# Moving three steps of an attention trunk by one slot: the value product, the sums of squares, the last heads

## The chip, the cores and the metric

The kernel runs on one core of one Trainium2 chip. Its engines are TensorE (PE: matmuls, transposes by matmul), ScalarE (ACT), VectorE (DVE), GpSimd (POOL) and SyncE (SP), which starts the transfers. Each engine works through its own queue in order. The metric is the time of one execution on the device in microseconds; lower is better.

## What is computed

Two pre-norm residual layers over 512 positions of width 2048, in float32. Layer 0 is an attention in which a small indexer scores all causal keys and each query attends to the best 128. Layer 1 is a block attention, which at this length comes to plain causal attention over 512 keys. Both have 16 query heads of width 128 that share 4 key and value heads, with a norm and a rotation of queries and keys, and a gate. Cut to what matters:

```python
def dsa_mixer(h, w_in, q_g, k_g, w_out):
    q, k, v, gate, qi, ki, wi = split_cols(h @ w_in, A_WIDTHS)
    q = rope(rms_norm(q.reshape(B, T, N_HEADS, HEAD_DIM), q_g), pos)
    k = rope(rms_norm(k.reshape(B, T, N_KV_HEADS, HEAD_DIM), k_g), pos)
    ...
    logits = jnp.einsum('bqgrd,bqkgd->bqgrk', qb, k_sel).astype(jnp.float32) * scale
    logits = jnp.where(valid[:, :, None, None, :], logits, NEG)
    p = jax.nn.softmax(logits, axis=-1).astype(v.dtype)
    o = jnp.einsum('bqgrk,bqkgd->bqgrd', p, v_sel)
    ...
    return (jax.nn.silu(gate) * o) @ w_out
```

## The kernel before

**The grid of slots.** All large matmuls are projections. Each makes a tile of 128 output columns (one head of `q`, `k`, `v` or the gate `g`, or 128 columns of an output projection `o0_n`, `o1_n`) for all 512 positions, and is cut into four quarters of four input tiles. A quarter is a unit: `products` (L184) issues 12 matmuls for it, since each float32 factor is split into a high and a low part and three products are kept (L193 high by high, L194 high by low, L195 low by high). The main loop goes over 484 units; the index of the unit is the slot. In slot i it splits the weights of unit i + 2 (`split`, L172: ACT casts the high part `whi`, DVE or GpSimd subtracts the low part `wlo`; three buffers each), starts loads, issues the 12 matmuls of unit i, perhaps starts the scores of a head (`maybe_attend`, L531), and then runs what was set for this slot with `later(k, f)`, that is k slots after the call.

**What sets the order.** On TensorE and SP the program's order stands as written. On ACT, DVE and GpSimd a scheduler orders the instructions after the opening part, so there a step can stand before or after its neighbours of other slots.

**Tiles and their steps.** When the four quarters of a tile are done, `done` sets its steps. A key tile (`k_tile`, L302) squares the result and cuts the squares into three bf16 parts (`Norm`, names `sq`, `b`), sums them over the head by 12 small matmuls (`sums`, name `cs`), makes the scale (`s3`, GpSimd's power), turns it into rows by four transposes (`bcast`, L224, name `b_k`), and multiplies the rotated keys by it (`s5`, DVE, name `t_k`), which then are cut into `kh` and `kl`. A query tile (L371) does the same without the row step: its scale `sc` goes into the softmax, so the scores need `q` alone, and the softmax needs `sc`. A value tile (L343) is scaled and then turned by four transposes (`s2`, L355, name `tv_v`). In each of the four groups of a layer a key tile, a value tile and four query tiles follow each other, with the gates between.

**One small bank.** `psm` (L123) gives the results of `sums`, `bcast` and the value tile's transposes a tile with the tag `sm`, which has one buffer.

**A head.** `attend` (L434) issues 12 score matmuls. Counted in slots from there: softmax at 1 (`soft`: on DVE the mask, `S<-s,mask`, on ACT the exponent), the division and a 32 by 32 turn on DVE at 2 (`u`), a transfer out at 3 and back at 4 (`leave`, `back`, names `d`, `pt`), the casts into `ph` (ACT) and `pl` (DVE) at 6, the value product `pv` (15 matmuls, L512, name `o`) at 8, the gate (`og`) at 9 and its low part at 10. `u` and `ph` share a tag with one buffer. The scores of a head start four slots or more after its query tile is done and 7 or 8 slots after those of the head before.

Of the kernel before, what the change touches and what calls it, by code (L numbers as in the profile page):

```python
# [37 lines left out]
HEADS = 16  # L38
# [55 lines left out]
def build(tc, a):  # L94
# [15 lines left out]
    def t512(tag, name, dt=F32, bufs=None, p=None, cols=T):  # L110
        return (p or kp).tile([P, cols], dt, tag=tag, name=name, **({"bufs": bufs} if bufs else {}))
# [4 lines left out]
    def small(tag, name, bufs=2):  # L116
        return kp.tile([P, NQ], F32, tag=tag, name=name, bufs=bufs)
# [13 lines left out]
    now = [0]  # L131
    SPLIT = 2

    def later(k, f, first=False):
        fs = hooks.setdefault(now[0] + k, [])
        fs.insert(0 if first else len(fs), f)
# [62 lines left out]
    def add(t, quarters=range(4)):  # L199
        units.extend((t, q) for q in quarters)  # L200
# [23 lines left out]
    def bcast(col, name):  # L224

        t = psm(name)
        for j in range(NQ):
            nc.tensor.transpose(t[:, j * P:(j + 1) * P], col[:, j:j + 1].to_broadcast([P, P]), ident)
        return t

    def cut_hi(hi, src):
        nc.scalar.copy(hi, src)

    def cut_lo(lo, src, hi):
        dve.tensor_tensor(lo, src, hi.bitcast(F32), op=OP.subtract)
# [28 lines left out]
    def rope(z, g, name):  # L264

        t1 = tmp(f"t1_{name}")
        t2 = tmp(f"t2_{name}")
        dve.scalar_tensor_tensor(t1, z, g, cos, op0=OP.mult, op1=OP.mult)
        for o, i in ((0, 64), (64, 0)):
            dve.scalar_tensor_tensor(t2[o:o + 64], z[i:i + 64], g[i:i + 64], sin[i:i + 64],  # L270
                                           op0=OP.mult, op1=OP.mult)
        dve.tensor_tensor(t1, t1, t2, op=OP.add)
        return t1
# [28 lines left out]
    def k_tile(Y, g):  # L302
        n = f"k{Y.L}_{g}"
        early = Y.L == 0 and g == 1
        v = SimpleNamespace()

        def s1():
            v.n = Norm(v.z, n)
            v.r = rope(v.z, Y.kg, n)

        def s2():
            v.n.middle()

        def s2b():
            v.s = v.n.sums()

        def s3():
            u = small("u", f"u_{n}")
            dve.scalar_tensor_tensor(u, v.s, 1.0 / P, Y.ce, op0=OP.mult, op1=OP.add)
            v.rk = small("rk", f"rk_{n}", 1)  # L320
            gps.tensor_tensor(v.rk, u, mhalf, op=OP.pow)

        def s4():
            v.b = bcast(v.rk, f"b_{n}")

        def s5():
            dve.tensor_tensor(v.r, v.r, v.b, op=OP.mult)
            p, th, tl = (bp, "bh15", "bl15") if early else (kp, "kh", "kl")
            kh = t512(th, f"kh_{n}", F32R, p=p)
            kl = t512(tl, f"kl_{n}", F32R, p=p)  # L330
            cut_hi(kh, v.r)
            Y.K[g] = (kh, kl)

        def s6():
            cut_lo(Y.K[g][1], v.r, Y.K[g][0])

        def done(z):
            v.z = z
            for k, f in ((1, s1), (2, s2), (3, s2b), (4, s3), (5, s4), (6, s5), (7, s6)):
                later(k, f)  # L340
        add(Tile(n, Y.w[16 + g], Y.X, done))

    def v_tile(Y, g):  # L343
# [27 lines left out]
    def q_tile(Y, h):  # L371
        n = f"q{Y.L}_{h}"
        early = Y.L == 0 and h < 8
        v = SimpleNamespace()

        def s1():
            v.n = Norm(v.z, n)
            v.r = rope(v.z, Y.qg, n)

        def s2b():  # L380
            v.s = v.n.sums()

        def s2():
            v.n.middle()
            p, th, tl = (bp, f"bh{9 - h % 4}", f"bl{9 - h % 4}") if early else (kp, "qh", "ql")
            qh = t512(th, f"qh_{n}", F32R, p=p)
            ql = t512(tl, f"ql_{n}", F32R, p=p)
            cut_hi(qh, v.r)
            cut_lo(ql, v.r, qh)
            Y.q[h] = (qh, ql)  # L390

        def s3():
            u = small("u", f"u_{n}")
            dve.tensor_tensor(u, v.s, Y.cq, op=OP.add)
            sc = small("sc", f"sc_{n}", 6)
            gps.tensor_tensor(sc, u, mhalf, op=OP.pow)
            Y.sc[h] = sc

        def done(z):
            v.z = z  # L400
            Y.qslot[h] = now[0]
            for k, f in ((1, s1), (2, s2), (3 + early, s2b), (4 + early, s3)):
                later(k, f)
        add(Tile(n, Y.w[h], Y.X, done))

    def g_tile(Y, h):
# [27 lines left out]
    def attend(Y, h):  # L434
# [53 lines left out]
        def cuts(hi, lo):  # L488
            if 0 in hi:
                v.ph = t512("ph", f"ph{n}", F32R, cols=1280)  # L490
                v.pl = t512("pl", f"pl{n}", F32R, cols=1280)
            for i in hi:
                o = slice(640 * i, 640 * i + 640)
                cut_hi(v.ph[:, o], v.t[:, o])
            for i in lo:
                o = slice(640 * i, 640 * i + 640)
                cut_lo(v.pl[:, o], v.t[:, o], v.ph[:, o])
# [27 lines left out]

        later(1, soft, True)
        for k, f in ((2, norm), (2, turn), (3, leave), (4, back),
                     (6, lambda: cuts((0, 1), (0, 1))), (8, pv), (9, gate), (10, rest)):
            later(k, f)

    def maybe_attend(Y):  # L531
        h = Y.head
        apart = 7 if h >= HEADS - 2 or (Y.L == 0 and h < 12) else 8
        if h < HEADS and Y.open and h in Y.qslot and now[0] >= Y.qslot[h] + 4 and now[0] >= Y.slot + apart:
            Y.head, Y.slot = h + 1, now[0]
            attend(Y, h)

# [281 lines left out]
    for i in range(len(units)):  # L819
        now[0] = i  # L820
        if i == OPENING:
            opening.close()
        dve.slot(i * SLOT)
        gps.slot(i * SLOT)
        if i in (2, 4):
            take_x(i // 2 + 1)
        split(i + SPLIT)
        if i == 0:
            take_x(1)
        if i in (0, 1):  # L830
            load(i + SPLIT, 1)
            load_x(i + 2)
        load(i + SPLIT)
        if i == 1:
            for n, t in (("cosi", cosi), ("sini", sini), ("cos", cos), ("sin", sin)):
                nc.sync.dma_start(t, a[n])
        products(i)
        maybe_attend(A if i < second else B)
        pending = hooks.get(i, [])
        while pending:  # L840
            pending.pop(0)()
        while fill and dve.until < (i + 1) * SLOT - SPARE:
            fill.pop(0)()
    for i in sorted(k for k in hooks if k >= len(units)):
        now[0] = i
        maybe_attend(B)
        for f in hooks[i]:
            f()
# [51 lines left out]
```

## Time and profile before

| | us |
|---|---|
| time, median of 3 runs | 1522.53 (1520.85 to 1524.11) |
| the profiled execution's own time | 1524.55 |
| its span, first to last instruction | 1522.8 |
| busy: TensorE, DVE, ACT, GpSimd | 1488.4, 916.5, 694.9, 145.5 |

The profile is of one execution. The busy times say which engine the span is made of. The table of waits says how long an engine sat idle and what ended that. The timeline has instructions in order of time: the start, how long it took, engine, line, operation, out<-in, and in square brackets the idle time before it and who ended it. A timeline row that ends in xN merges N instructions. Matmuls overlap, so the distance of two starts is what one costs, not its length. PEclk is the granted clock of TensorE, 1.00 for 2.4 GHz and 0.50 for 1.2 GHz. The lines L77 on DVE and GpSimd are a helper that issues all their operations: there the names tell them apart.

### The profile page before, as it was taken

To read this page: it belongs to the slowest core of one execution; us is meant where nothing else is said; L and a number is where in the kernel's file an instruction comes from. 1 tells how busy PE (TensorE), PEld (TensorE's weight loads), DVE (VectorE), ACT (ScalarE), POOL (GpSimd) and SP (SyncE) were. 2 spreads that over 40 slices of the span, in tenths; PEclk is the share of its full clock that TensorE was granted. 3 is DMA by queue.
4 is the path that set the end of the run, shared out by engine and by line. 5 is a ranking of instruction groups with operands and counts; after the bars stand their busy time and mean duration, and the time that the engine had idled before them with its cause. 6 is when DMAs were issued, how large, how long until landed. Compare 5 with 4: busy or idle time off the path is not lost.

```text
span 1522.8 us, 20238 instructions
## 1 busy us (share of the span) xinstructions
PE 1488.4 (98%) x7348; PEld 1243.2 (82%) x7348; DVE 916.5 (60%) x1848; ACT 694.9 (46%) x1332; POOL 145.5 (10%) x128
## 2 busy tenths in 40 slices
PE   9999999999998999999999999999999999999999
PEld 6998888878777788888888888888888888888887
DVE  5898966665666556653334565667666666643332
ACT  6874334544455435443333454455444545542221
POOL 0433540000000000001111000000000000000000
PEclk9999999999999999999999999999999999999999
DMA  7332224343344424354443244343425343354442
GB/s 244 106 97 84 85 96 139 118 142 115 108 135 128 128 70 135 115 180 145 146 145 132 84 135 136 114 121 104 153 84 152 104 132 104 122 156 166 145 145 90
DMA packets 72677, 191.79 MB, mean 126 GB/s; under 512 B 8192, under 2 KB 25344, under 8 KB 72576
## 3 DMA queue, kind: packets, MB, share of 16 engines
q1 hardware_dynamic: 72576, 190.50, 39.8%
q8 instruction: 57, 0.93, 0.3%
q14 instruction: 44, 0.36, 0.1%
HBM read 161.11 MB, written 29.36 MB: 125 GB/s over the span
## 4 chain that ended last, share of the span: by engine, by line
PE 64%; ACT 2%; DVE 1%; issue 1%; DVEq 0%; ACTq 0%
PE z_o L193 8%; PE z_o L195 8%; PE z_o L194 8%; PE z_g L193 5%; PE z_q L193 5%; PE z_q L194 5%; PE z_g L195 5%; PE z_g L194 5%; PE z_q L195 5%; PE o L512 3%; PE z_v L193 1%; PE z_k L193 1%; PE z_k L194 1%; PE z_k L195 1%; PE z_v L195 1%; PE z_v L194 1%
## 5 line engine op out<-in xcount | busy, mean ns | idle before, releaser
L193 PE MATMUL z_q<-xh,whi_q 128*128 128x512 f32 x512 | 203.8, 398 | 0.0
L193 PE MATMUL z_g<-xh,whi_g 128*128 128x512 f32 x512 | 202.7, 396 | 0.0
L195 PE MATMUL z_q<-xh,wlo_q 128*128 128x512 f32 x512 | 200.7, 392 | 0.0
L194 PE MATMUL z_q<-xl,whi_q 128*128 128x512 f32 x512 | 200.7, 392 | 0.0
L195 PE MATMUL z_g<-xh,wlo_g 128*128 128x512 f32 x512 | 199.8, 390 | 0.0
L194 PE MATMUL z_g<-xl,whi_g 128*128 128x512 f32 x512 | 199.3, 389 | 0.0
L193 PE MATMUL z_o<-bh,whi_o 128*128 128x512 f32 x512 | 199.3, 389 | 0.0
L195 PE MATMUL z_o<-bh,wlo_o 128*128 128x512 f32 x512 | 199.2, 389 | 0.0
L194 PE MATMUL z_o<-bl,whi_o 128*128 128x512 f32 x512 | 199.2, 389 | 0.0
L77 DVE TENSOR_TENSOR wlo_o<-raw_o,whi_o 128x512 fp32r<-128x512 f32 x128 | 88.8, 694 | 159.6 <-ACT whi_o L179 159.6
L179 ACT CAST whi_o<-raw_o 128x512 fp32r<-128x512 f32 x128 | 79.8, 624 | 225.6 <-PE z_o L194 215.9
L179 ACT CAST whi_g<-raw_g 128x512 fp32r<-128x512 f32 x128 | 79.4, 620 | 172.3 <-PE z_q L194 122.8
L179 ACT CAST whi_q<-raw_q 128x512 fp32r<-128x512 f32 x128 | 79.3, 620 | 159.1 <-PE z_q L194 74.2
L77 DVE TENSOR_TENSOR wlo_g<-raw_g,whi_g 128x512 fp32r<-128x512 f32 x112 | 76.7, 686 | 107.2 <-ACT whi_g L179 106.9
L77 DVE TENSOR_TENSOR wlo_q<-raw_q,whi_q 128x512 fp32r<-128x512 f32 x114 | 77.6, 684 | 63.9 <-ACT whi_q L179 58.7
L195 PEld LDWEIGHTS z_q<-xh,wlo_q 128*128 128x128 f32 x512 | 96.8, 189 | 20.9
L195 PEld LDWEIGHTS z_g<-xh,wlo_g 128*128 128x128 f32 x512 | 96.1, 188 | 20.9
L194 PEld LDWEIGHTS z_q<-xl,whi_q 128*128 128x128 f32 x512 | 97.1, 190 | 19.1
L193 PEld LDWEIGHTS z_q<-xh,whi_q 128*128 128x128 f32 x512 | 97.1, 190 | 19.0
L195 PEld LDWEIGHTS z_o<-bh,wlo_o 128*128 128x128 f32 x512 | 96.1, 188 | 20.1
L194 PEld LDWEIGHTS z_o<-bl,whi_o 128*128 128x128 f32 x512 | 96.1, 188 | 20.1
L193 PEld LDWEIGHTS z_o<-bh,whi_o 128*128 128x128 f32 x512 | 96.1, 188 | 19.6
(167 smaller groups left out, 2733.3 us busy)
## 6 DMA issues: line engine op xcount, KB each, us to landing
d<-u SPq DMA_DIRECT2D x32, 640.0 KB, 3.2
pt<-d SPq DMA_DIRECT2D x128, 160.0 KB, 4.0
raw_q<-w_a SPq DMA_DIRECT2D x32, 512.0 KB, 3.9
raw_g<-w_a SPq DMA_DIRECT2D x32, 512.0 KB, 3.9
raw_q<-w_b SPq DMA_DIRECT2D x32, 512.0 KB, 3.7
raw_g<-w_b SPq DMA_DIRECT2D x32, 512.0 KB, 3.6
raw_o<-w_ao SPq DMA_DIRECT2D x26, 512.0 KB, 3.6
raw_o<-w_bo SPq DMA_DIRECT2D x26, 512.0 KB, 3.6
```

What stands on the lines that cost most here:

```text
L77: return f(out, *args, **kw)
L179: nc.scalar.copy(hi, r)
L193: nc.tensor.matmul(o, lhsT=hi[:, k], rhs=xh, start=kt == 0, stop=False)
L194: nc.tensor.matmul(o, lhsT=hi[:, k], rhs=xl, start=False, stop=False)
L195: nc.tensor.matmul(o, lhsT=lo[:, k], rhs=xh, start=False, stop=kt == KT - 1)
L512: nc.tensor.matmul(o[:, q], lhsT=l[:, kt * P:kt * P + P], rhs=r[:, t], start=m == 0 and c == 0, stop=m == 4 and c == 2)
```

## The change

The steps of a key tile after the cutting of squares move one slot later (sums 4, scale 5, rows 6, product 7, low part 8); the sums and the scale of a query tile stand at 4 and 5, where the first eight query tiles of layer 0 stood already. Scores start five slots or more after their query tile instead of four. The value product stands nine slots after the scores instead of eight, gate and low part follow. The last three heads instead of the last two are seven slots apart.

```diff
         def done(z):
             v.z = z
-            for k, f in ((1, s1), (2, s2), (3, s2b), (4, s3), (5, s4), (6, s5), (7, s6)):
+            for k, f in ((1, s1), (2, s2), (4, s2b), (5, s3), (6, s4), (7, s5), (8, s6)):
                 later(k, f)
         add(Tile(n, Y.w[16 + g], Y.X, done))
...
             Y.qslot[h] = now[0]
-            for k, f in ((1, s1), (2, s2), (3 + early, s2b), (4 + early, s3)):
+            for k, f in ((1, s1), (2, s2), (4, s2b), (5, s3)):
                 later(k, f)
...
         for k, f in ((2, norm), (2, turn), (3, leave), (4, back),
-                     (6, lambda: cuts((0, 1), (0, 1))), (8, pv), (9, gate), (10, rest)):
+                     (6, lambda: cuts((0, 1), (0, 1))), (9, pv), (10, gate), (11, rest)):
             later(k, f)
...
-        apart = 7 if h >= HEADS - 2 or (Y.L == 0 and h < 12) else 8
-        if h < HEADS and Y.open and h in Y.qslot and now[0] >= Y.qslot[h] + 4 and now[0] >= Y.slot + apart:
+        apart = 7 if h >= HEADS - 3 or (Y.L == 0 and h < 12) else 8
+        if h < HEADS and Y.open and h in Y.qslot and now[0] >= Y.qslot[h] + 5 and now[0] >= Y.slot + apart:
```

On ACT, around the casts `ph` of head 5 in layer 0, whose value product stood after unit `k0_2_2` and now stands after `k0_2_3` (the two units before `v0_2_0`), there was this row:

```order
L415 ACTIVATE th_g0_7_3753<-gz_g0_7_3751 128x512
L179 CAST whi_k0_2_3_3755<-raw_k0_2_2_3566 128x512
L179 CAST whi_v0_2_0_3790<-raw_v0_2_0_3671 128x512
L179 CAST whi_v0_2_1_3838<-raw_v0_2_0_3671 128x512
L232 CAST ph0_5_3745<-pt0_5_3662 128x640 x2
L460 ACTIVATE S0_6_3806,sm0_6_3807<-S0_6_3806,nb0_6_3809,sc_q0_6_3387 128x512
```

and on the same engine and place there is now:

```order
L415 ACTIVATE th_g0_7_3753<-gz_g0_7_3751 128x512
L179 CAST whi_k0_2_3_3755<-raw_k0_2_2_3566 128x512
L179 CAST whi_v0_2_0_3790<-raw_v0_2_0_3666 128x512
L232 CAST ph0_5_3745<-pt0_5_3657 128x640 x2
L179 CAST whi_v0_2_1_3822<-raw_v0_2_0_3666 128x512
L179 CAST whi_v0_2_2_3868<-raw_v0_2_2_3714 128x512
```

`ph` moved ahead of one cast of weights, and the product that reads it moved back by one unit.

On TensorE, at the third key tile of layer 1, whose scale is turned into rows by `b_k1_2`, the matmuls stood in this order (`tv_v1_2`, the value tile's transposes, came after nine more matmuls of `z_q1_8`):

```order
L195 MATMUL z_q1_8_10283<-xh1_3_6695,wlo_q1_8_0_10213 128x512
L228 MATMUL b_k1_2_10301<-ident_80,rk_k1_2_10277 128x128 x4
L193 MATMUL z_q1_8_10283<-xh1_4_6775,whi_q1_8_1_10241 128x512
L194 MATMUL z_q1_8_10283<-xl1_4_6776,whi_q1_8_1_10241 128x512
L195 MATMUL z_q1_8_10283<-xh1_4_6775,wlo_q1_8_1_10242 128x512
```

and now, after the value product of head 7:

```order
L512 MATMUL o1_7_10300<-pl1_7_10223,vh_v1_1_9132 128x256
L512 MATMUL o1_7_10300<-pl1_7_10223,vh_v1_1_9132 128x128
L228 MATMUL b_k1_2_10316<-ident_80,rk_k1_2_10278 128x128 x4
L355 MATMUL tv_v1_2_10321<-ident_80,vt_v1_2_10280 128x128 x4
L193 MATMUL z_q1_8_10263<-xh1_8_7107,whi_q1_8_2_10259 128x512
```

The two sets of transposes, both into the tag `sm`, moved next to each other; so they stand at all eight key tiles.

On DVE, ahead of the product `t1_k0_2` of the third key tile of layer 0, which reads `b_k0_2`, there stood:

```order
L77 SCALAR_TENSOR_TENSOR u_k0_2_3983<-cs_k0_2_3946,ce0_1380 128x4
L77 TENSOR_TENSOR vt_v0_2_4024<-z_v0_2_3877,rstd0_1448 128x512
L77 TENSOR_TENSOR wlo_q0_8_2_3988<-raw_q0_8_2_3842,whi_q0_8_2_3987 128x512
L77 TENSOR_TENSOR wlo_q0_8_3_4027<-raw_q0_8_2_3842,whi_q0_8_3_4026 128x512
L77 TENSOR_TENSOR t1_k0_2_3899<-t1_k0_2_3899,b_k0_2_4019 128x512
L77 TENSOR_TENSOR pl0_6_3978<-pt0_6_3872,ph0_6_3977 128x640 x2
```

and now:

```order
L77 TENSOR_TENSOR wlo_q0_9_0_4066<-raw_q0_9_0_3908,whi_q0_9_0_4065 128x512
L77 ISA S0_7_4039,mx0_7_4041<-s0_0_7_4000,mask_93 128x512
L77 ISA mx0_7_4041 128x1
L77 ISA S0_7_4039,mx0_7_4041<-s1_0_7_4001,mask_93 128x384
L77 ISA mx0_7_4041 128x1
L77 SCALAR_TENSOR_TENSOR nb0_7_4042<-mx0_7_4041,sc_q0_7_3644 128x1
L77 ISA S0_7_4039,mx0_7_4041<-s1_0_7_4001,mask_93 128x128
L77 ISA mx0_7_4041 128x1
L77 SCALAR_TENSOR_TENSOR nb0_7_4042<-mx0_7_4041,sc_q0_7_3644 128x1
L77 ISA S0_7_4039,mx0_7_4041<-s2_0_7_4002,mask_93 128x256
L77 TENSOR_TENSOR t1_k0_2_3898<-t1_k0_2_3898,b_k0_2_4055 128x512
```

The masking of the scores of head 7 moved ahead of the key tile's product.

## Rows read from the trace of the kernel before

**Rows 1.** The page: busy time, share, instructions; the chain of waits by engine.

```profile
PE 1488.4 (98%) x7348; PEld 1243.2 (82%) x7348; DVE 916.5 (60%) x1848; ACT 694.9 (46%) x1332; POOL 145.5 (10%) x128
PE 64%; ACT 2%; DVE 1%; issue 1%; DVEq 0%; ACTq 0%
```

**Rows 2.** Waits of TensorE: line <- releaser: us in total, times, longest.

```profile
PE o L512 <- ACT ph L232: 18.6, 14, 2.1
PE cs_q L298 <- DVE b_q L77: 2.6, 4, 0.7
PE cs_k L298 <- ACT b_k L291: 1.3, 1, 1.3
...
PE cs_q L298 <- ACT b_q L291: 1.0, 1, 1.0
PE cs_k L298 <- DVE b_k L77: 1.0, 1, 1.0
PE o L512 <- DVE pl L77: 0.8, 1, 0.8
```

**Rows 3.** Stretches after waits: busy PE, PEld, DVE, ACT, POOL; PEclk, DMA share, GB/s.

```profile
298.90:302.20 3.30, 3.30 (x13) 3.01 (x13) 2.60 (x13) 2.05 (x7) 0.00 (x0) 0.50 0.00 0
...
374.60:377.90 3.30, 3.30 (x21) 3.09 (x22) 3.27 (x14) 1.02 (x3) 0.00 (x0) 1.00 0.58 164
...
531.00:534.30 3.30, 3.30 (x11) 2.72 (x10) 1.51 (x3) 0.62 (x1) 0.00 (x0) 0.50 0.01 5
```

**Rows 4.** Timeline of TensorE: two neighbours at low clock; one place in two quarters.

```profile
391.33 0.63 PE L193 MATMUL z_v<-xh,whi_v 128*128 128x512 f32 x1
391.76 0.63 PE L194 MATMUL z_v<-xl,whi_v 128*128 128x512 f32 x1
...
875.37 0.39 PE L193 MATMUL z_g<-xh,whi_g 128*128 128x512 f32 x1
...
878.09 0.39 PE L193 MATMUL z_g<-xh,whi_g 128*128 128x512 f32 x1
```

**Rows 5.** Timeline of ACT and of TensorE, layer 0, head 5.

```profile
372.66 0.62 ACT L179 CAST whi_v<-raw_v 128x512 fp32r<-128x512 f32 x1 [3.98 <-PE z_k L194]
373.19 1.35 ACT L232 CAST ph<-pt 128x640 fp32r<-128x640 f32 x2
...
374.58 0.87 PE L512 MATMUL o<-ph,vh_v 128*128 128x256 f32 x5 [1.73 <-ACT ph L232]
```

**Rows 6.** Timeline of ACT and of TensorE, layer 1, head 4.

```profile
1025.52 0.62 ACT L287 CAST b_q<-sq_q 128x512 bf16<-128x512 f32 x1
1026.05 1.34 ACT L232 CAST ph<-pt 128x640 fp32r<-128x640 f32 x2
...
1027.44 0.51 PE L512 MATMUL o<-ph,vh_v 128*128 128x256 f32 x2 [0.97 <-ACT ph L232]
```

**Rows 7.** Timeline of TensorE and of DVE, second key tile of layer 1.

```profile
979.76 0.60 PE L228 MATMUL b_k<-ident,rk_k 128*128 128x128 f32 x4
...
980.44 0.69 DVE L77 TENSOR_TENSOR wlo_q<-raw_q,whi_q 128x512 fp32r<-128x512 f32 x1 [1.21 <-ACT whi_q L179]
981.05 0.68 DVE L77 TENSOR_TENSOR t_k<-t_k,b_k 128x512 f32<-128x512 f32 x1
...
982.98 0.60 PE L355 MATMUL tv_v<-ident,vt_v 128*128 128x128 f32 x4
```

**Rows 8.** Timeline of TensorE and of DVE, first key tile of layer 0.

```profile
134.98 0.61 PE L228 MATMUL b_k<-ident,rk_k 128*128 128x128 f32 x4
...
135.63 0.69 DVE L77 TENSOR_TENSOR t_k<-t_k,b_k 128x512 f32<-128x512 f32 x1 [0.82 <-PE b_k L228]
```

**Rows 9.** Timeline of DVE: masking of a head's scores, first step and next work.

```profile
402.81 0.68 DVE L77 CUSTOM_DVE_ANT_0 S<-s,mask 128x512 f32<-128x512 f32 x1
...
404.66 0.69 DVE L77 TENSOR_TENSOR wlo_q<-raw_q,whi_q 128x512 fp32r<-128x512 f32 x1
```

**Rows 10.** Timeline of DVE: the gate after a value product.

```profile
1107.37 0.69 DVE L77 SCALAR_TENSOR_TENSOR og<-o,gu_g 128x512 f32<-128x512 f32 x1 [0.73 <-PE o L512]
```

**Rows 11.** Timeline of DVE: the turn of a head's softmax.

```profile
880.92 1.69 DVE L77 STREAM_TRANSPOSE u<-S 128x320 f32<-128x320 f32 x4 [1.47 <-ACT S L467]
```

## The prediction

> **What bounds the kernel now.** I read the busy times and the chain of waits first. TensorE is busy for 98% of the span, and in the chain the shares of the other engines are 2% and less [rows 1]. So the kernel is a stream of matmuls, and only two things can shorten it without taking matmuls away: the moments in which TensorE waits, and the moments in which its clock is low. The table of TensorE's waits comes next [rows 2]. Outside the opening (before 80 us, which the change doesn't touch) it holds two families. The value products `o` wait for their casts `ph`, 18.6 us in 14 of 32 heads, and once for `pl`, 0.8 us. The sums of squares `cs` wait for their bf16 parts, 2.6 + 1.3 + 1.0 + 1.0 = 5.9 us in 7 waits. Together 25.3 us. Then the clock: five stretches run at a granted clock of 0.50, 1.2 instead of 2.4 GHz, and each follows waits of these two families [rows 3], which show the first and the last of the five, and the stretch after one equally long wait, which ran at 1.00.
>
> **Why the value product waits.** In layer 0 the product of six heads waits 1.73 to 2.06 us; [rows 5] show one. ACT's cast of the weights of the unit three places further on, `whi_v`, starts only at 372.66, when TensorE has left the buffer, since there are three; `ph` stands behind it and starts at once when ACT is free, so its transfer had landed. ACT is idle before, but in order. TensorE has nothing between: it waits out both casts, 0.62 + 1.35 us less an overlap. In layer 1 seven heads, and one late head of layer 0, wait 0.97 us in another way: the squares `sq_q` and `b_q` of a query tile that has just ended stand ahead of `ph` [rows 6], and the scores of the next head cover half of that.
>
> **The change, part by part.**
> *Value product one slot later.* A slot is twelve matmuls, 2.72 us, as the same matmul of two quarters shows [rows 4]. The casts stay at six slots after the scores, so the product gains up to 2.72 us on its casts, more than any of the 14 waits. But ACT's order is made anew, so I compared what stands ahead of each `ph` with where its product stands. For 13 of the 14 heads the last cast ahead waits for a unit that ends at least one unit before the product. The nearest cases keep about 2.72 - (0.62 + 1.35 - 0.1) = 0.8 us. Head 11 of layer 0 doesn't gain: its `ph` moved back behind `whi_q0_12_1`, which again waits for the very unit after which the product stands. I keep 1.8 us for it, the middle of the six [rows 2, 5]. Gone: 18.6 + 0.8 - 1.8 = 17.6 us.
> *Sums one slot later.* All seven waits are at most 1.3 us, less than a slot; all are on tiles that move (the first eight query tiles of layer 0 were at four already). Gone: 5.9 us. The scale that follows now exists at five slots, so the scores wait for five, which moves most of the scores by one slot. No engine gets more work, and the transfers `leave` and `back` keep their distance from the scores on SP.
> *The key tile's later steps, one slot later.* This is where I expect the price. The transposes `b_k` now stand at the tile's end plus 6. The value tile ends four slots after the key tile and transposes at plus 2: the same slot. Both write the PSUM tag `sm`, which has one buffer. Before, twelve matmuls lay between, and `tv_v` started 1.25 us after DVE had read `b_k` (981.05 + 0.68 to 982.98) [rows 7], so that wait cost nothing. Now `tv_v` follows `b_k` directly, and TensorE must wait until DVE's `t_k` has read the buffer, at all eight key tiles. The price is the time from the end of `b_k` to the end of `t_k`. Before, it was 0.73 us where DVE was free (135.63 + 0.69 less 134.98 + 0.61) [rows 8] and 1.37 us where one `wlo` stood ahead (981.73 less 980.36) [rows 7]. In the new order, three tiles have one `wlo` ahead, which in turn waits for ACT: 1.35 us each. Three (layer 1, the later groups) have `og` of the value product ahead, 0.69 us [rows 10], but that starts when the product ends, while `b_k` runs: 0.95 us each. The first tile has steps of the top-k search ahead, 1.5 us. The third has a `wlo` and the whole masking of a head's scores ahead: 0.62 for the cast `whi`, 0.60 for `wlo`, 1.85 for the masking (402.81 to 404.66) [rows 9], 0.7 for `t_k`, less 0.6 for `b_k`: 3.2 us. Added: 3 x 1.35 + 3 x 0.95 + 1.5 + 3.2 = 11.6 us. Bounds: all eight with DVE free, 8 x 0.73 = 5.8 us; seven at 2.0 us (cast, `wlo` and `t_k` in a row) and the one of 3.2, 17.2 us.
> A rule of the Trainium skill (Perfetto Trace Analysis, section Matmuls) speaks against this part: independent matmul groups should rotate through different PSUM banks, so that one group's evacuation runs beside the next group's matmuls. The 1.25 us of room before [rows 7] agrees that one bank does while other matmuls lie between; by the rule alone, with a second bank, the 11.6 us would fall away and the time would be about 1497.
> *Last three heads seven apart.* This takes back the one slot for the heads 13 to 15, so the last scores of each layer stand where they stood. The last head's product is one slot later; its cut ends some 2 us after it (three steps of 0.6 to 0.7 us), and TensorE asks for it after two more units and nine matmuls, over 7 us later. No cost.
> *Clock.* At the low clock a matmul takes 0.43 us instead of 0.23 (391.33 to 391.76; 2.72 over 12) [rows 4], and about eight fall in a stretch: 1.6 us each, five are 8.0 us. Waits of 1.0 us and less were never followed by one, lone waits of 1.7 to 2.1 us in three of five cases, two close waits of over 2.2 us in sum both times. After the change I count one for the 3.2 us, 0.6 for the 1.8 us, 0.2 each for the four of about 1.4 us: with a little for the rest 2.5, so 4.0 us are gained. Bounds: one stretch (6.4 us gained) and six (1.6 us lost).
>
> **The sum.** The profiled execution took 1524.55 us around its span of 1522.8. 1524.55 - 17.6 - 5.9 + 11.6 - 4.0 = 1508.65. It lies 2.0 us above the median of the three runs, about one low-clock stretch; I don't subtract that, since a run after the change can have one stretch more or less just as well. Forecast 1508.7 us, by itself 1503 to 1514.
>
> **The rivals.**
> *The key tiles' waits are short.* If DVE's queue is freer there than in the order, each wait is near 0.73 us: 1508.7 - 5.8 = 1502.9. For it: three of the eight had this before. Against: the new queue has work ahead of `t_k` at every tile.
> *The value product waits again.* Seven heads (the last head of the first three groups in layer 1, head 13 of both layers, heads 9 and 10 of layer 0) have 0.8 us of room. If transfers land later than they did, or a cast more slips ahead, about 1 us comes back at each: 1515.7. Against: in [rows 5] `ph` waited for ACT, not for its data.
> *The clock falls after every new wait.* Nine waits, each with a stretch of 1.6 us: 14.4 instead of 4.0, so 1519.1. For it: a fall at 1.74 + 0.84 us. Against: two lone waits of 1.73 and 2.06 us without.
> *Slower than before.* `u` of the next head and `ph` share one buffer, and with seven slots between heads (16 places) the transposes of the next head now stand in the slot of the product and must wait until it ends; behind them in DVE's queue stand the weight cuts `wlo`. From the end of the product DVE needs 1.69 us [rows 11] + 0.69, and TensorE asks for that `wlo` after 2.72 + 0.45 us: 0.8 us of room, where a slot more was before. It decides once about 0.8 us of other DVE work gets between; with 2 us more at each place TensorE would lose 1.2 x 16 = 19 us: 1527.9. Against: DVE is busy for 60% [rows 1], and such an excess everywhere isn't in the order.
> That the change doesn't do what it says is excluded for TensorE, whose order is written by hand; for ACT and DVE it is the second rival.
>
> **How the numbers follow.** Forecast 62%, short waits 13%, product waits 12%, clock 8%, slower 5%. The range 1501 to 1517 takes in the first three with their bounds and leaves out the last two and a little of each edge. About 0.2%, 3 us, is what a measurement of this kernel tells from no change: faster means below 1519.5, slower above 1525.6. The clock rival lies just inside faster, half of its weight counts as same. Faster 0.91, same 0.05, slower 0.04.
>
> **What would show it.** Right: `o` waiting for `ph` once, by about 1.8 us, in head 11 of layer 0; no waits of `cs`; a new row in the waits of TensorE, `tv_v` for `t_k`, 8 times, 10 to 13 us in sum, longest above 3 us at the third key tile; one to four stretches at 0.50. Wrong: `o` waiting more than three times, `tv_v` hardly at all, matmuls `z` waiting for `wlo`, or more than five stretches at 0.50.

## The result and the profile after

The changed kernel takes 1502.87 us (median of 4 runs, 1502.25 to 1504.17), the kernel before 1522.42 us beside it: a ratio of 0.9872 with a 95% interval of 0.9855 to 0.9890, 19.5 us faster. The profiled execution of the changed kernel took 1502.38 us, with a span of 1500.6.

The busy row of the page and the row under the chain of waits answer to [rows 1]:

```profile
PE 1479.2 (99%) x7348; PEld 1238.3 (83%) x7348; DVE 917.0 (61%) x1848; ACT 694.7 (46%) x1332; POOL 146.7 (10%) x128
PE 94%; DVE 2%; DMA 1%; ACT 1%; issue 1%; SPq 0%; POOL 0%; DVEq 0%; ACTq 0%; POOLq 0%
```

The number of instructions is the same on each of these engines. TensorE is busy for 9 us less although it does the same work: about 6.4 us of that are matmuls that ran at the low clock before, and about 2.1 us come from how a matmul before a wait is shown (both are worked out below). The waits of TensorE (us in total, times, longest) answer to [rows 2]:

```profile
PE tv_v L355 <- DVE t_k L77: 11.6, 8, 3.2
PE o L512 <- ACT ph L232: 1.7, 1, 1.7
PE cold L808 <- DVE idle L77: 1.3, 1, 1.3
PE is L658 <- DVE Q L77: 1.2, 1, 1.2
```

The last two rows are of the opening and were there before. Of the two families of before, one wait of `o` is left and none of `cs`. In their place stands a wait that the kernel before didn't have at all: the value tile's transposes `tv_v`, eight times, until DVE has read the key tile's rows. The longest is at the third key tile of layer 0. The timeline there (start, length, engine, line, operation, idle time before):

```profile
391.15 0.62 ACT L179 CAST whi_q<-raw_q 128x512 fp32r<-128x512 f32 x1 [2.40 <-PE z_q L194]
...
391.18 0.60 PE L228 MATMUL b_k<-ident,rk_k 128*128 128x128 f32 x4
...
391.80 0.69 DVE L77 TENSOR_TENSOR wlo_q<-raw_q,whi_q 128x512 fp32r<-128x512 f32 x1 [2.09 <-ACT whi_q L179]
392.41 0.68 DVE L77 CUSTOM_DVE_ANT_0 S<-s,mask 128x512 f32<-128x512 f32 x1
...
394.27 0.68 DVE L77 TENSOR_TENSOR t_k<-t_k,b_k 128x512 f32<-128x512 f32 x1
...
395.00 0.77 PE L355 MATMUL tv_v<-ident,vt_v 128*128 128x128 f32 x3 [3.22 <-DVE t_k L77]
```

`b_k` is done at 391.78, but DVE first waits for ACT's cast, cuts the weights and masks a head's scores for 1.86 us; `t_k` ends at 394.95 and TensorE goes on at once. The second key tile of layer 1, the place of [rows 7], shows the short form, with the gate `og` ahead of `t_k`:

```profile
964.00 0.61 PE L228 MATMUL b_k<-ident,rk_k 128*128 128x128 f32 x4
...
964.20 0.69 DVE L77 SCALAR_TENSOR_TENSOR og<-o,gu_g 128x512 f32<-128x512 f32 x1 [0.78 <-PE o L512]
964.81 0.68 DVE L77 TENSOR_TENSOR t_k<-t_k,b_k 128x512 f32<-128x512 f32 x1
...
965.54 0.44 PE L355 MATMUL tv_v<-ident,vt_v 128*128 128x128 f32 x2 [0.93 <-DVE t_k L77]
```

The clock, in stretches that begin after a wait as in [rows 3] (busy time of PE, PEld, DVE, ACT, POOL, then PEclk, DMA share, GB/s):

```profile
395.30:398.60 3.30, 3.30 (x11) 2.71 (x10) 1.47 (x3) 3.30 (x10) 0.00 (x0) 0.50 0.00 0
...
519.30:522.60 3.30, 3.30 (x21) 3.07 (x22) 1.49 (x3) 0.49 (x1) 0.00 (x0) 1.00 0.49 159
532.00:535.30 3.30, 3.30 (x17) 2.77 (x18) 1.38 (x2) 1.18 (x3) 0.00 (x0) 1.00 0.00 1
```

Only the wait of 3.22 us was followed by a stretch at 0.50 (1.2 GHz); the one of 1.74 us and the ones of about 1.4 us were not.

### The profile page after: what moved, and what is told of

Same layout as the page of the kernel before. It is cut to its first block, busy times and chain, and to the rows that moved or that the text cites. A ratio compares the mean times of both kernels' runs of the same rounds, so it can differ in the third digit from the quotient of the medians.

```text
span 1500.6 us, 20234 instructions
## 1 busy us (share of the span) xinstructions
PE 1479.2 (99%) x7348; PEld 1238.3 (83%) x7348; DVE 917.0 (61%) x1848; ACT 694.7 (46%) x1332; POOL 146.7 (10%) x128
## 4 chain that ended last, share of the span: by engine, by line
PE 94%; DVE 2%; DMA 1%; ACT 1%; issue 1%; SPq 0%; POOL 0%; DVEq 0%; ACTq 0%; POOLq 0%
PE z_g L193 8%; PE z_q L193 8%; PE z_g L195 8%; PE z_o L193 8%; PE z_g L194 8%; PE z_o L195 8%; PE z_o L194 8%; PE z_q L194 8%; PE z_q L195 8%; PE o L512 4%; PE z_k L193 2%; PE z_k L195 2%; PE z_k L194 2%; PE z_v L193 2%; PE z_v L194 2%; PE z_v L195 2%
```

## The experiments

The theory is that of the prediction: the gain is the value product's and the sums' waits, and the loss is one small bank with two users in one slot. The rivals are that the parts earn something else than was forecast for them, and that DVE's late `t_k` would hold up TensorE wherever it is read. Each kernel was timed beside the kernel before; the ratios are to that.

**The value product alone.** The kernel before with only these two edits:

```diff
-                     (6, lambda: cuts((0, 1), (0, 1))), (8, pv), (9, gate), (10, rest)):
+                     (6, lambda: cuts((0, 1), (0, 1))), (9, pv), (10, gate), (11, rest)):
-        apart = 7 if h >= HEADS - 2 or (Y.L == 0 and h < 12) else 8
+        apart = 7 if h >= HEADS - 3 or (Y.L == 0 and h < 12) else 8
```

> The value product alone is moved (nine slots behind the scores, last three heads seven apart); sums, scales and the key tile's rows stand as before. Theory (the shared small bank is what the moved sums cost): tv_v waits for t_k not at all, o waits for ph once by about 1.7 us, cs waits stay at 4 to 6 us; 1522.4 - 17.7 for o - about 2 for the part of each wait that its idle row doesn't show - 4 to 6 for the clock = 1497 to 1499, faster than the full change at 1502.9. Rival (the eight waits of tv_v come with the later value product, and the sums paid for themselves): tv_v still waits 11.6 us, cs 5.9 us come back, 1509.

Measured: 1498.92 us, ratio 0.9860 (0.9844 to 0.9876). The median is 4 us below that of the whole change; by the ratios it is 2 us, and their intervals overlap. Its waits of TensorE after the opening:

```profile
PE cs_q L298 <- DVE b_q L77: 3.1, 4, 1.4
PE o L512 <- ACT ph L232: 1.8, 1, 1.8
...
PE cs_q L298 <- ACT b_q L291: 1.2, 2, 0.6
...
PE cs_k L298 <- DVE b_k L77: 0.5, 1, 0.5
PE cs_k L298 <- ACT b_k L291: 0.2, 1, 0.2
```

`tv_v` doesn't wait, the sums do, for 5.0 us, and the clock is low in three stretches, two of them behind waits of the sums. So the value product, with the last three heads, earns by itself at least as much as the whole change, and the new wait belongs to the moved sums and key tile steps, as the theory has it.

**The sums alone.** The other half: the two tuples of the tiles and the five slots between query tile and scores, with the last three heads seven apart, but the value product at eight.

```diff
-            for k, f in ((1, s1), (2, s2), (3, s2b), (4, s3), (5, s4), (6, s5), (7, s6)):
+            for k, f in ((1, s1), (2, s2), (4, s2b), (5, s3), (6, s4), (7, s5), (8, s6)):
-            for k, f in ((1, s1), (2, s2), (3 + early, s2b), (4 + early, s3)):
+            for k, f in ((1, s1), (2, s2), (4, s2b), (5, s3)):
...
-        ... now[0] >= Y.qslot[h] + 4 ...
+        ... now[0] >= Y.qslot[h] + 5 ...
```

> The sums of squares, their scales and the key tile's rows alone are moved (and the scores to five slots after their query tile, last three heads seven apart); the value product stays eight slots behind the scores. Theory: cs waits gone (5.9 us), tv_v waits 11 to 12 us, o waits for its casts at 18 us or more; slower than before, 1527 to 1535. Rival (the later sums are a gain by themselves): 1516.

Measured: 1533.70 us, ratio 1.0093 (1.0074 to 1.0112), slower. Its waits:

```profile
PE o L512 <- ACT ph L232: 20.2, 12, 2.3
PE tv_v L355 <- DVE t_k L77: 10.6, 8, 1.5
PE o L512 <- DVE pl L77: 5.0, 6, 0.8
```

The sums' waits are gone; `tv_v` waits; and the value product waits longer than before, and at other heads. In layer 1 the heads 3, 7 and 11 now wait about 1.73 us each, and the heads 0, 1, 4, 5, 8 and 9 wait 0.82 us for `pl` instead of 0.97 us for `ph`. At head 3 of layer 1, `ph` (976.75) again follows at once on a cast of weights (976.23) that TensorE released. Why the scheduler put it there wasn't traced.

**The last three heads alone.** This is one edit, the `apart` line of the first experiment, on the kernel before.

> The kernel before, with the last three heads seven slots apart instead of the last two, and nothing else. Theory (a head seven slots after another meets a cast of weights three units on ahead of its ph while the product is at eight slots): in both layers o of head 13 waits about 1.7 us, cs of the last two query tiles waits some 2.5 us more, against 0.97 us that head 12 no longer waits; 4 to 7 us slower than before. Rival (that part costs nothing by itself, as the prediction took it): the time of the kernel before.

Measured: 1533.09 us, ratio 1.0074 (1.0048 to 1.0099): 10.7 us slower than the 1522.36 beside it, more than expected. Its waits:

```profile
PE o L512 <- ACT ph L232: 20.1, 14, 2.1
PE cs_q L298 <- ACT b_q L291: 3.7, 3, 1.7
PE cs_q L298 <- DVE b_q L77: 3.7, 6, 0.7
```

Against [rows 2], `o` waits 1.5 us more and `cs_q` 2.7 + 1.1 us more, 5.3 us in sum. Two more stretches run at the low clock than in the profile of before, seven instead of five, one late in each layer (3.2 us). Four added waits each cost 0.16 us more than the idle time that the table counts (worked out below), 0.6 us. Together that is 9.1 us, the difference of the two profiled spans (1531.9 and 1522.8). The place is head 13, in layer 0 here:

```profile
615.00 0.62 ACT L179 CAST whi_g<-raw_g 128x512 fp32r<-128x512 f32 x1 [4.01 <-PE z_q L194]
615.53 1.35 ACT L232 CAST ph<-pt 128x640 fp32r<-128x640 f32 x2
...
616.93 0.51 PE L512 MATMUL o<-ph,vh_v 128*128 128x256 f32 x2 [1.74 <-ACT ph L232]
```

That is the pattern of [rows 5]: `ph` stands behind a cast of weights that waits for the unit just ahead of the product. So this part isn't free by itself; beside the later product head 13 doesn't wait. The opposite, the whole change with two heads seven apart, wasn't tried: there, by the order of the program, the last head's low part would be issued behind the matmuls that read it.

**The value tile one slot later.** The whole change, and the value tile moved as well, which puts twelve matmuls between `b_k` and `tv_v` again:

```diff
         def done(z):
             v.z = z
-            for k, f in ((1, s1), (2, s2), (3, s3)):
+            for k, f in ((1, s1), (3, s2), (4, s3)):
                 later(k, f)
         add(Tile(n, Y.w[20 + g], Y.X, done))
```

> The full change, and the value tile's transposes and cuts one slot later too (3 and 4 instead of 2 and 3), so that twelve matmuls lie again between b_k and tv_v. Theory (one bank, two users in one slot): no wait of tv_v, nothing in its place, 1502.9 - 11.6 - 8 x 0.16 - 1.6 for the one stretch of low clock = 1488 to 1491. Rival (DVE is late with t_k and will hold up TensorE somewhere else, at the next sums or at kh): about 1500.

Measured: 1489.79 us, ratio 0.9803 (0.9784 to 0.9823). All that is left after the opening, in its table of waits:

```profile
PE o L512 <- ACT ph L232: 1.9, 2, 1.7
...
PE cs_q L298 <- DVE b_q L77: 0.8, 1, 0.8
```

and the second key tile of layer 1, shown above for the changed kernel, in its timeline:

```profile
954.70 0.61 PE L228 MATMUL b_k<-ident,rk_k 128*128 128x128 f32 x4
...
955.51 0.68 DVE L77 TENSOR_TENSOR t_k<-t_k,b_k 128x512 f32<-128x512 f32 x1
...
957.89 0.38 PE L355 MATMUL tv_v<-ident,vt_v 128*128 128x128 f32 x2
```

`t_k` ends 0.88 us after `b_k`, no sooner than in the changed kernel (965.49 against 964.61). So it is at seven of the eight key tiles: `t_k` ends as late behind `b_k` as in the changed kernel, to 0.01 us, and nothing waits for it. That rules out the rival there: what cost was the shared bank at a distance of no matmul. At the third key tile of layer 0 DVE's order is another one, without the masking ahead (`b_k` from 388.54 for 0.60 us, `t_k` from 389.77 for 0.68 us): `t_k` ends 1.31 us after `b_k` instead of 3.17, so no run here shows what 3.17 us would cost with matmuls between. The largest delay that stayed hidden is 2.61 us, at the second key tile of layer 0 in the run with the value product alone; `tv_v` starts 0.05 us after it there, so one unit of room was just enough. A second buffer for the tag `sm` wasn't tried.

**The key tile put back.** The whole change with the key tile's tuple as before, the query tiles' kept:

```diff
-            for k, f in ((1, s1), (2, s2), (4, s2b), (5, s3), (6, s4), (7, s5), (8, s6)):
+            for k, f in ((1, s1), (2, s2), (3, s2b), (4, s3), (5, s4), (6, s5), (7, s6)):
```

> The full change with the key tile's steps put back to 3, 4, 5, 6, 7; the query tiles' sums stay later, and so do the value product and the scores. Theory (it is the key tile's rows in the value tile's slot that cost, not the sums): no wait of tv_v, cs_k waits under 1 us at one tile, 1488 to 1491. Rival (the key tile's sums need the later slot): cs_k waits of 2 to 3 us come back, with a low clock after them, 1493 to 1495.

Measured: 1490.09 us, ratio 0.9791 (0.9767 to 0.9815). Its waits after the opening:

```profile
PE o L512 <- ACT ph L232: 1.7, 1, 1.7
...
PE cs_k L298 <- DVE b_k L77: 0.6, 1, 0.6
PE cs_q L298 <- DVE b_q L77: 0.4, 1, 0.4
PE cs_k L298 <- ACT b_k L291: 0.3, 1, 0.3
```

`tv_v` waits nowhere, `cs_k` for 0.8 us in two steps at one tile. So the key tile's part of the change is what costs here.

**Head 11 of layer 0.** Both repairs were run once more with the value product of that one head a slot later:

```diff
+        far = Y.L == 0 and h == 11
         later(1, soft, True)
...
-                     (6, lambda: cuts((0, 1), (0, 1))), (9, pv), (10, gate), (11, rest)):
+                     (6, lambda: cuts((0, 1), (0, 1))), (9 + far, pv), (10 + far, gate), (11 + far, rest)):
```

> As the one before, and the value product of head 11 of layer 0 alone stands ten slots behind its scores. Theory (its ph stands in ACT's queue behind the cast of the weights three units on, so one slot more frees it): the last o wait of 1.7 us goes, 2 us less than the kernel before this one, 1486 to 1489; no stretch of low clock in the middle. Rival (the cast follows the product wherever it goes): the wait stays at 1.7 us and the time with it.

> As the one before, and head 11 of layer 0 with its value product ten slots behind its scores. Theory: the o wait of 1.7 us goes too, 1486 to 1489, level with the version that moved the value tile instead. Rival: moving the value tile is better by the cs_k wait, 2 us and more.

Measured: 1487.44 us with the later value tile, ratio 0.9785 (0.9769 to 0.9800), and 1488.37 us with the key tile put back, ratio 0.9781 (0.9752 to 0.9810). The wait of 1.7 us is gone in both. The two repairs are level: the ratios differ by far less than their intervals. Either is faster than both kernels of this case, some 13 to 15 us below the changed one.

**The parts added up.** From the ratios, in one order of steps, with the kernel before as 1522 us: the heads +0.0074, the value product on top 0.9860 - 1.0074 = -0.0214, the query tiles' sums on top 0.9791 - 0.9860 = -0.0069, the key tile's steps on top 0.9872 - 0.9791 = +0.0081. That is +11, -33, -11 and +12 us, with an uncertainty of 4 to 5 us each. Taken as the last step instead, on top of the run with the sums alone, the value product gives 0.9872 - 1.0093 = -0.0221, the same within that. The 11 us of the query tiles' sums are only in part waits. Between the profiles of the value product alone and of the key tile put back, the spans differ by 9.3 us and the idle rows by 3.9 (6.9 and 3.0); five waits at 0.16 us are 0.8, and three stretches of low clock, at 1.6 us each, are 4.8.

## Why the prediction was right, and by how much it was off

- **The value product.** It said that 13 of 14 waits go and head 11 of layer 0 keeps about 1.8 us. One wait of 1.74 us was left, in that head. Right, and by the mechanism that was named: ACT's queue has a cast `whi_q` there that waits for the unit `z_v` just ahead of the product, and `ph` follows it.

```profile
517.26 0.62 ACT L179 CAST whi_q<-raw_q 128x512 fp32r<-128x512 f32 x1 [1.52 <-PE z_v L194]
517.78 1.35 ACT L232 CAST ph<-pt 128x640 fp32r<-128x640 f32 x2
```

- **The sums.** All seven waits gone, as forecast.
- **The key tiles.** 11.6 us in 8 waits were forecast and measured. The single prices were 3.2 at the third tile (3.22 measured), 1.5 at the first (1.48), 1.35 at three (1.37, 1.41 and 1.37) and 0.95 at three (0.93 each). The durations came from [rows 7 to 10], and what stands ahead of `t_k` from the order.
- **The last heads.** "No cost" holds for the whole change, where neither head 13 nor the last query tiles wait. It doesn't hold for this part by itself: alone it costs 10.7 us.
- **The clock.** Here the term was mis-sized. 2.5 stretches were forecast, the profile has one: none after the wait of 1.74 us (counted 0.6) and none after the four of 1.4 us (0.2 each). At the 1.6 us per stretch of the sum that is 2.4 us too little gain. The 0.6 was a chance, drawn once, and settles little: the same head's wait of 1.79 us in the run with the value product alone did have a stretch behind it. The 0.2 each looks too high: in the profiles of the changed kernel and of the sums alone, none of thirteen lone waits of 1.36 to 1.48 us was followed by one. The price itself agrees with another estimate. The kernel before was run 14 times beside the experiments, at granted clocks from 0.999 (1517.2 to 1519.0 us, 4 runs) to 0.993 (1524.7 us). Its profile at 0.994 has five stretches, so 0.999 is about one (the changed kernel's profile, with one stretch, is at 0.999), and four stretches make (1524.55 - 1518) / 4 = 1.6 us each.
- **A term left out.** The sum priced a wait by its idle row. In the changed kernel the last matmul before the one wait of `o` starts at 517.06 and `o` at 519.19 (the rows below): 2.13 us, where 0.23 is usual, so 1.90 us are lost, and the idle row says 1.74.

```profile
517.06 0.39 PE L195 MATMUL z_v<-xh,wlo_v 128*128 128x512 f32 x1
519.19 0.51 PE L512 MATMUL o<-ph,vh_v 128*128 128x256 f32 x2 [1.74 <-ACT ph L232]
```

A matmul is shown as 0.39 us long but costs 0.23 when the next one follows; a wait uncovers the other 0.16. There were 22 waits after the opening and there are 9: 13 x 0.16 = 2.1 us more gain.

Against the spans: 1522.8 - 1500.6 = 22.2 us. The idle rows after the opening fell by 11.9 us (25.3 to 13.4), the uncovered tails by 2.1, four stretches of low clock are 6.4, and the opening, whose instructions the change doesn't move, ran 1.1 us shorter in this execution (the first `z_k` starts at 103.35 instead of 104.41; in the seven other profiles between 103.79 and 104.33). Together 21.5; the 0.7 left isn't traced. The forecast of 1508.7 was 6.3 us above the profiled execution's 1502.38 (5.8 above the median): 2.4 for the clock, 2.1 for the tails, 1.1 for the opening, which the change doesn't touch, and the 0.7. All four point the same way, so no error hid another; the waits themselves were forecast to 0.1 us. The measured 1502.87 lies just below the 1503 to 1514 that was given for the forecast by itself, and inside the whole range of 1501 to 1517, near its lower end.

The rivals: the short key tile waits didn't happen, although the measured time is just the one forecast for them (1502.9), so the time alone would have pointed to the wrong cause and only the table of waits tells the two apart; the product's return didn't happen; the clock's fall after every new wait didn't, in none of the four runs (granted clock 0.998 and 0.999); and the slower case, DVE's turn held up by the product, left no trace: no matmul `z` waits for `wlo` after the opening.

## What to carry to other kernels

Where queues are filled by hand on one engine and by a scheduler on others, read for each waiting matmul which earlier entry of the releasing engine's queue itself waits for the matmuls just ahead; one slot of distance then frees it, and the order of both kernels shows in advance where it doesn't. When a step is moved by a slot, look for what else writes the same single buffer in its new slot: here eight collisions took back 12 of some 32 us, and moving the other user by the same slot removed them. And take a chain of moves apart before keeping it: of the four parts here the value product earned 33 us and the query tiles' sums 11, the other two cost 11 and 12, and one of these two, the key tile's, could be dropped.

## What the runs showed of the hardware

The low clock is not a property of the kernel alone. The same kernel before had runs at a mean granted clock from 0.993 to 0.999 and times from 1517.2 to 1524.7 us that follow it. Lone waits of 1.7 to 2.1 us were followed by a stretch at 1.2 GHz in some executions and places and not in others: in the profile of the sums alone, where nine waits lie between 1.7 and 2.3 us, three of them. The one wait over 3 us was. So was, in the run with the value product alone, a pair of waits of 0.57 and 0.98 us that end 1.15 us apart (granted clock 0.50 from 409.20 to 412.50). The prediction's count, by which no wait of 1.0 us or less and only pairs of over 2.2 us in sum were followed by one, is true of the kernel before and doesn't carry over to this one. In the profiles of the two repairs and their variants with head 11, no stretch in the middle of the span ran low. Part of what a change gains by removing waits is therefore a number of such stretches, and it differs from run to run by several microseconds.
